# Gate bias and log-sigmoid taken 272 columns wide at the array, and scan operands written twice by the row loads

## Chip, core and metric

The kernel runs on one core of one Trainium2 chip, in float32. The metric is the device time of one execution in microseconds. Before the change it is 1172.42 us, the median of three runs (1170.26 to 1176.19).

In this text PE is TensorE, PEld its weight loads, DVE VectorE, ACT ScalarE, POOL GpSimd and SP the queue of SyncE that issues DMAs.

## The reference

One layer of a decoder trunk in which two groups of heads work side by side, followed by a final RMSNorm. There are 1024 prompt tokens and 8 sequences of 8 sample tokens, 1088 columns in all; the model width is 1024. Cut to what matters:

```python
xn   = rmsnorm(x, g_norm)
xm, zm, om, fh, qh, ih, zh = split(xn @ w_in)          # seven blocks of 1024 columns
xc   = silu(causal_conv(xm))                           # mLSTM group: 4 heads
q, k, v = xc_h @ w_q, xc_h @ w_k, xm_h @ w_v
gates = concat[q, k, v] @ w_gate + b_gate              # 8 numbers a token
ig, lf = gates[:, :4], log_sigmoid(gates[:, 4:])       # input gate, log of the forget gate
hm   = mlstm_scan(q, k, v, ig, lf)                     # b = cumsum(lf); m = running max
hm   = (layernorm(hm) * sigmoid(om) + m_skip * xc) * silu(zm)
oh   = hgrn2_scan(silu(qh), 1 - f, ih, log f)          # HGRN2 group: 8 heads, f from fh
oh   = rmsnorm(oh) * silu(zh)
y    = rmsnorm(x + concat[hm, oh] @ w_out)             # and the new states
```

The scan of the mLSTM needs, for each head, the row m over the tokens with m(t) = max(m(t-1) + lf(t), ig(t)), and the running sum b of lf. For the sample tokens each of the eight sequences starts anew from its own state.

## The kernel before

A float32 matmul is made of three passes over operands that are split in a high and a low part (`mm3`, lines 94 to 96: high times high, low times high, high times low). x is normalised, transposed and split into `XH` and `XL` once. W_in is read in blocks of 128 columns: for each, `in_block` loads the weights (`wraw`, line 140), casts them on ACT (`whi`) and subtracts on POOL or DVE (`wlo`, line 147), and multiplies them in three chunks of 384, 384 and 320 columns (PSUM tile `mm`, three buffers), each of which an evac function takes out.

The front does the eight xm blocks: convolution, q, k and v of the four mLSTM heads, and the gates. `gate_part` (L101 o<-qk,front) multiplies q and k of a head by the gate weights so that the result lies in four groups of 32 partitions: partition 32 j + r holds gate r (0 to 3 input, 4 to 7 forget) of columns 272 j to 272 j + 271. DVE adds the heads up in `GT`, columns 688 to 959 of the tile `front` (line 445). After the last head `gate_scan` makes the gate rows, and the trunk begins.

The trunk runs twelve jobs: H0, M0, H1, M1, H2, M2, H3, M3, H4 to H7. While the scan of one job runs (`hgrn_main` or `mlstm_main`), the input blocks of a following one (f, q, i, z of an H, om and zm of an M) are woven between its matmuls. `weave` deals them out: each `yield` of a main part states a time, and so much matmul work, times a ratio, is put in behind it. The ratio is the cost of a job's blocks divided by `HEAD` plus an `extra`. The order of PE is then fixed as written; that of the other engines comes from a scheduler that simulates times while the program is built. Each engine and each queue works strictly in its order.

In H0's stretch the input blocks are, in order, q, i and z of H0 itself and then om of M0. H0's own scan first forms Q, K and a burst of small matmuls (lv<-Q,K, line 101), then DVE forms seven levels of products (`products`: QK<-hq,f, line 1026; the levels 2, 4, 8 are one burst lv<-QK, the levels 16, 32, 64 the upper burst), DVE copies the results through masks into A (line 984 and 987), ACT copies A on (lines 1068 and 1075), and PE transposes KD (line 1132).

`gate_scan` is a generator: its first part runs at the end of the front, the others within H0's main part (`with_gates`). Before the change the first part stores `GT` to DRAM (`gd`, line 557), loads it back as two tiles with one head in a partition, `ig` and `y` (tile name gy, four partitions by 1088 columns, line 560), and adds the bias (line 561). The second part takes the log-sigmoid on ACT (lines 563 to 565) and DVE (line 566, `lf`, tile glf), copies `lf` to `t1` (tile gt) and `ig` to `y` (lines 571, 573), puts the sequence starts in, and scans m (line 575, tile gm). The third runs the second scan, b (line 583). `lm`, line 570, is the start of the sample sequences.

Of the kernel before, what the change touches and what calls it, by code (L numbers as in the profile page):

```python
# [15 lines left out]
P = 128  # L16
# [14 lines left out]
def hybrid_step(  # L31
# [276 lines left out]
    rd = dp.tile([4, T], F32, name="rd")  # L308
    mixd = dp.tile([15, P, T], F32, name="mixd")
    y0d = dp.tile([T, 512], F32, name="y0d")  # L310
    gd = dp.tile([P, 272], F32, name="gd")


    PAR = cp.tile([P, NPAR], F32, name="PAR")
# [231 lines left out]
        gate_part(h, parts, last)  # L546

    COLS = cp.tile([P, 9, 8], F32, name="COLS")
    bgt = cp.tile([4, 2], F32, name="bgt")
    m0t = cp.tile([4, 8], F32, name="m0t")  # L550
    nc.sync.dma_start(out=bgt, in_=b_gate[0].rearrange("(g h) -> h g", g=2))
    nc.sync.dma_start(out=m0t, in_=st_m[0].rearrange("b h -> h b"))

    def gate_scan():

        ig, y, lf, t1, m, b = [unit(s)[0:4, :T] for s in ("ig", "gy", "glf", "gt", "gm", "gb")]
        nc.sync.dma_start(out=gd, in_=GT)
        gv = gd.rearrange("(j r) t -> r j t", r=32)
        for g, dst in ((0, ig), (1, y)):
            nc.sync.dma_start(out=dst.rearrange("p (j t) -> p j t", t=272), in_=gv[4 * g:4 * g + 4])  # L560
            V.tensor_scalar(dst, dst, scalar1=bgt[:, g:g + 1], scalar2=None, op0=ALU.add)
        yield 1.0
        S.activation(t1, y, AF.Abs)
        S.activation(t1, t1, AF.Exp, scale=-1.0)
        S.activation(t1, t1, AF.Ln, bias=1.0)
        V.scalar_tensor_tensor(lf, y, 0.0, t1, op0=ALU.min, op1=ALU.subtract)
        lfs = lf[:, TP:T].rearrange("p (b c) -> p b c", c=8)[:, :, 0]
        igs = ig[:, TP:T].rearrange("p (b c) -> p b c", c=8)[:, :, 0]
        lm = small(8, "lm")
        V.tensor_tensor(lm[0:4, :], lfs, m0t, op=ALU.add)  # L570
        V.tensor_copy(t1, lf)
        V.memset(t1[:, TP:T].rearrange("p (b c) -> p b c", c=8)[:, :, 0], -1e30)
        V.tensor_copy(y, ig)
        V.tensor_tensor(y[:, TP:T].rearrange("p (b c) -> p b c", c=8)[:, :, 0], igs, lm[0:4, :], op=ALU.max)
        V.tensor_tensor_scan(m, t1, y, initial=0.0, op0=ALU.add, op1=ALU.max)
        yield 6.5
        G.memset(t1, 1.0)
        G.memset(t1[:, 0:TP].rearrange("p (b c) -> p b c", c=P)[:, :, 0], 0.0)
        G.memset(t1[:, TP:T].rearrange("p (b c) -> p b c", c=8)[:, :, 0], 0.0)
        st = lf[:, 0:TP].rearrange("p (b c) -> p b c", c=P)[:, 1:8, 0]  # L580
        V.tensor_tensor(st, st, m[:, 0:TP].rearrange("p (b c) -> p b c", c=P)[:, 0:7, 127], op=ALU.add)
        V.tensor_copy(lfs, lm[0:4, :])
        V.tensor_tensor_scan(b, t1, lf, initial=0.0, op0=ALU.mult, op1=ALU.add)
        V.tensor_tensor(y, b, m, op=ALU.subtract)
        nc.sync.dma_start(out=rd, in_=y)
        V.tensor_tensor(ig, ig, b, op=ALU.subtract)
        nc.sync.dma_start(out=o_pm[0, 0].unsqueeze(1), in_=m[:, TP - 1:TP])
        msl = small(8, "msl")
        V.tensor_copy(msl[0:4, :], m[:, TP:T].rearrange("p (b c) -> p b c", c=8)[:, :, 7])
        nc.sync.dma_start(out=o_sm[0].rearrange("b h -> h b"), in_=msl[0:4, :])  # L590
        yield 6.5
        ps = ps_o()
        for t in range(8):
            PE.transpose(ps[:, t * 8:t * 8 + 4], ig[:, t * P:t * P + P], ident[0:4, 0:4])
            PE.transpose(ps[:, t * 8 + 4:t * 8 + 8], m[:, t * P:t * P + P], ident[0:4, 0:4])
        for j in range(4):
            for o, src in ((64, ig), (68, m)):
                PE.matmul(ps[32 * j:32 * j + 32, o:o + 4], lhsT=src[:, TP + win(j):TP + win(j) + 32],
                          rhs=ident[0:4, 0:4], start=True, stop=True)
        V.tensor_copy(COLS.rearrange("p a b -> p (a b)"), ps[:, :72])  # L600
        S.activation(COLS[:, :, 4:8], COLS[:, :, 4:8], AF.Exp, scale=-2.0)
        yield 0.5

        co = unit("co")
        for kk in range(2):
            pt = ps_o()
            for k in range(4):
                PE.transpose(pt[:27, k * P:(k + 1) * P], CS[:, kk * 4 + k, :], ident)
            V.tensor_copy(co[:27, kk * 512:(kk + 1) * 512], pt[:27, :])
        nc.sync.dma_start(out=o_pconv[0, 0], in_=co[0:3, :DM])  # L610
        nc.sync.dma_start(out=o_sconv[0].rearrange("b j d -> (b j) d"), in_=co[3:27, :DM])
        yield 0.5
# [818 lines left out]
    with tc.manual_schedule(engines={mybir.EngineType.PE}):  # L1431
        for i, (kind, h) in enumerate(jobs[:-1]):
            main = (hgrn_main if kind == "H" else mlstm_main)(h)
            extra = 0.0
            if kind == "H" and i and jobs[i - 1][0] == "M":
                extra = 5.2
            if i == 0:
                main, extra = with_gates(main, gates), 14.0
            weave(islice(side, STEPS), main, us / (HEAD[kind] + extra))
        weave(side, hgrn_main(7), (us / 2 + EARLY * cost(45, 512)) / HEAD["H"])  # L1440
        for t in range(9):
# [100 lines left out]
```

## Time and profile before

| | |
|---|---|
| median of three runs | 1172.42 us (1170.26 to 1176.19) |
| profiled execution | 1167.87 us, its span 1166.1 us |
| mean granted TensorE clock | 0.992 |
| busy share of the span | PE 96%, PEld 91%, DVE 64%, ACT 40%, POOL 22% |
| gates, first to last instruction | 218.4 us (store of `gd`) to 278.9 us (COLS on ACT) |

The time of the profiled execution is its span and 1.8 us around it. A busy share is a mean over stages. A row of the timeline gives the start in us, the duration, the engine, the line of the kernel, the operation, the output and the inputs, and in brackets how long the engine had been idle before it and which work ended that.

### The profile page before, as it was taken

What the parts mean: (1) busy time and instruction counts of PE and PEld (TensorE: products, weight loads), DVE (VectorE), ACT (ScalarE), POOL (GpSimd) and SP (SyncE); (2) the same over time, 40 slices, a digit from 0 to 9 for tenths busy, and PEclk for the clock granted to TensorE, in tenths of its full rate; (3) what the DMA queues carried; (4) which work ended last, traced back from release to release, by engine and by line L of the source; (5) the groups of instructions that cost most, each with busy time, mean ns of one, the idle gap of its engine ahead of it and who ended that gap; (6) DMA issues with size and microseconds to landing.
All of it is one profiled execution on the core that took longest, in us unless ns stands there. A gap on an engine that the chain in (4) does not pass through costs nothing.

```text
span 1166.1 us, 22935 instructions
## 1 busy us (share of the span) xinstructions
PE 1124.4 (96%) x9251; PEld 1057.3 (91%) x9251; DVE 748.0 (64%) x1477; ACT 469.6 (40%) x1045; POOL 260.5 (22%) x402
## 2 busy tenths in 40 slices
PE   5889999998999999999999999999999999999997
PEld 5779999997999999999999999999999998878886
DVE  4665354485678657794679467878667586643543
ACT  5454454335532443235332553252423354343332
POOL 4352343101531044202530153102020200100000
PEclk9889999999999999999999999999999999999999
DMA  7234343213324242243224332322121155476662
GB/s 251 47 126 145 118 144 124 82 36 103 95 76 135 75 161 81 79 137 102 88 77 151 112 96 77 126 81 77 55 77 56 59 172 153 144 231 168 196 186 96
DMA packets 154060, 133.88 MB, mean 115 GB/s; under 512 B 11439, under 2 KB 130155, under 8 KB 153954
## 3 DMA queue, kind: packets, MB, share of 16 engines
q1 hardware_dynamic: 153954, 132.41, 36.5%
q8 instruction: 73, 1.20, 0.4%
q14 instruction: 33, 0.27, 0.1%
HBM read 93.96 MB, written 38.43 MB: 114 GB/s over the span
## 4 chain that ended last, share of the span: by engine, by line
PE 67%; ACT 4%; DMA 2%; DVE 2%; issue 1%; POOLq 0%; SPq 0%; DVEq 0%; ACTq 0%
PE mm L94 18%; PE mm L96 18%; PE mm L95 18%; PE lv L101 2%; ACT A L1075 1%; PE o L1178 1%; ACT A L1068 1%; PE o L1197 1%; DMA woraw<-in_w_out 1%; PE o L94 1%; PE o L95 1%; PE o L96 1%; PE o L1200 1%; DMA mraw<-mixd 1%; PE lv L712 1%
## 5 line engine op out<-in xcount | busy, mean ns | idle before, releaser
L94 PE MATMUL mm<-XH,whi 128*128 128x384 f32 (+1 forms) x1344 | 452.2, 337 | 3.2 <-DVE xml L470 2.0
L95 PE MATMUL mm<-XL,whi 128*128 128x384 f32 (+1 forms) x1344 | 440.6, 328 | 0.0
L96 PE MATMUL mm<-XH,wlo 128*128 128x384 f32 (+1 forms) x1344 | 440.1, 328 | 0.0
L94 PEld LDWEIGHTS mm<-XH,whi 128*128 128x128 f32 x1344 | 254.2, 189 | 6.9 <-DVE xml L470 2.2
L95 PEld LDWEIGHTS mm<-XL,whi 128*128 128x128 f32 x1344 | 254.3, 189 | 1.6 <-issue 1.3
L96 PEld LDWEIGHTS mm<-XH,wlo 128*128 128x128 f32 x1344 | 253.7, 189 | 0.0
L147 POOL TENSOR_TENSOR wlo<-wraw,whi 128x1024 fp32r<-128x1024 f32 x34 | 83.1, 2446 | 108.3 <-ACT whi L147 108.2
L147 ACT CAST whi<-wraw 128x1024 fp32r<-128x1024 f32 x56 | 58.8, 1051 | 104.8 <-PE mm L95 85.3
L944 POOL MEMSET A<- 128x288 f32 x8 | 2.7, 343 | 248.2 <-ACT A L1068 248.2
L94 PE MATMUL mm<-XH,mhi 128*128 128x512 f32 x144 | 57.2, 397 | 0.5 <-ACT mhi L1290 0.5
L96 PE MATMUL mm<-XH,mlo 128*128 128x512 f32 x144 | 56.3, 391 | 0.7 <-DVE mlo L1291 0.7
L95 PE MATMUL mm<-XL,mhi 128*128 128x512 f32 x144 | 56.1, 389 | 0.0
L1290 ACT CAST mhi<-mraw 128x1024 fp32r<-128x1024 f32 (+1 forms) x32 | 31.8, 997 | 60.1 <-PE mm L95 43.9
L1291 DVE TENSOR_TENSOR mlo<-mraw,mhi 128x1024 fp32r<-128x1024 f32 (+1 forms) x32 | 37.0, 1155 | 24.5 <-ACT mhi L1290 24.3
L892 DVE TENSOR_SCALAR f<-f,OML,LB 128x384 f32<-128x384 f32 (+1 forms) x24 | 33.8, 1407 | 28.5 <-ACT f L890 28.5
L470 DVE TENSOR_TENSOR xml<-mm,xmh 128x384 fp32r<-128x384 f32 (+1 forms) x24 | 12.3, 511 | 51.0 <-ACT XB L469 48.0
L1359 POOL TENSOR_TENSOR rs<-rs,mhalf 128x1 f32<-128x1 f32 (+1 forms) x9 | 4.9, 544 | 148.0 <-DVE rs L1358 148.0
L96 PE MATMUL mm<-woh,mlo 128*128 128x512 f32 x96 | 37.5, 390 | 0.4 <-DVE mlo L1291 0.4
L94 PE MATMUL mm<-woh,mhi 128*128 128x512 f32 x96 | 37.4, 389 | 0.0
L95 PE MATMUL mm<-wol,mhi 128*128 128x512 f32 x96 | 37.4, 389 | 0.0
L486 DVE SCALAR_TENSOR_TENSOR Y<-XB,PAR,Y 128x1112 f32<-128x1112 f32 x24 | 36.8, 1533 | 0.3
L199 POOL TENSOR_SCALAR oss<-oss 128x4 f32<-128x4 f32 (+1 forms) x24 | 4.6, 194 | 143.6 <-DVE oss L1148 143.6
(351 smaller groups left out, 2224.8 us busy)
## 6 DMA issues: line engine op xcount, KB each, us to landing
wraw<-in_w_in SPq DMA_DIRECT2D x56, 512.0 KB, 4.2
woraw<-in_w_out SPq DMA_DIRECT2D x16, 512.0 KB, 5.3
mraw<-mixd SPq DMA_DIRECT2D x16, 512.0 KB, 4.9
mraw<-mixd SPq DMA_DIRECT2D x16, 448.0 KB, 4.0
xcd<-XB SPq DMA_DIRECT2D x8, 544.0 KB
qkd<-qk SPq DMA_DIRECT2D x16, 272.0 KB, 3.5
xcr<-xcd SPq DMA_DIRECT2D x8, 544.0 KB
mixd<-xcr SPq DMA_DIRECT2D x8, 544.0 KB, 4.2
```

Of the source, the lines that this page charges most:

```text
L94: PE.matmul(out, lhsT=lh, rhs=rh, start=first, stop=False)
L95: PE.matmul(out, lhsT=lh, rhs=rl, start=False, stop=False)
L96: PE.matmul(out, lhsT=ll, rhs=rh, start=False, stop=last)
L101: i = PE.matmul(out, lhsT=lhsT, rhs=rhs, start=start, stop=stop)
L147: return S.copy(hi, raw), eng.tensor_tensor(lo, raw, f32(hi), op=ALU.subtract)
L470: evs.append(V.tensor_tensor(ml[:, t0:t0 + m], ps[:, :m], f32(mh[:, t0:t0 + m]), op=ALU.subtract))
L486: V.scalar_tensor_tensor(Y[:, :1112], XB[:, j:j + 1112], cw[:, 8 * j + ft:8 * j + ft + 1], Y[:, :1112], op0=ALU.mult, op1=ALU.add)
L712: PE.matmul(ps[:, u * P:(u + 1) * P], lhsT=k[:, j * P:(j + 1) * P], rhs=q[:, j * P:(j + 1) * P], start=True, stop=True)
L892: V.tensor_scalar(f[:, s], f[:, s], scalar1=OML[:, h:h + 1], scalar2=LB[:, h:h + 1], op0=ALU.mult, op1=ALU.add)
L1068: S.copy(dst, A32[32 * j:32 * j + 32, 0:256].rearrange("p (r e c) -> p r e c", e=2, c=32))
L1290: S.copy(hi[:, :w * n], raw[:, :w * n])
L1291: V.tensor_tensor(lo[:, :w * n], raw[:, :w * n], f32(hi[:, :w * n]), op=ALU.subtract)
```

## The change

Bias and log-sigmoid are taken on `GT` itself, where all eight gates of a quarter of the columns lie in one instruction of 272 columns on 128 partitions. The bias becomes a column of 128 partitions (`bgt`), filled by four loads of the eight numbers instead of one, after a memset to zero. The logs go to a new tile `lg`. `gd` holds two such tiles, gates and logs, and four loads instead of two write the rows: the logs to `lf` and to `t1`, the input gates to `ig` and to `y`. The two copies go. The stated times in `gate_scan` and the `extra` of H0 come down by 2.5.

```diff
-    gd = dp.tile([P, 272], F32, name="gd")
+    gd = dp.tile([2, P, 272], F32, name="gd")
...
-    bgt = cp.tile([4, 2], F32, name="bgt")
+    bgt = cp.tile([P, 1], F32, name="bgt")
+    G.memset(bgt, 0.0)
     m0t = cp.tile([4, 8], F32, name="m0t")
-    nc.sync.dma_start(out=bgt, in_=b_gate[0].rearrange("(g h) -> h g", g=2))
+    for j in range(4):
+        nc.sync.dma_start(out=bgt[32 * j:32 * j + 8, :], in_=b_gate[0].unsqueeze(1))
...
-        nc.sync.dma_start(out=gd, in_=GT)
-        gv = gd.rearrange("(j r) t -> r j t", r=32)
-        for g, dst in ((0, ig), (1, y)):
-            nc.sync.dma_start(out=dst.rearrange("p (j t) -> p j t", t=272), in_=gv[4 * g:4 * g + 4])
-            V.tensor_scalar(dst, dst, scalar1=bgt[:, g:g + 1], scalar2=None, op0=ALU.add)
+
+        lg = half("lg")
+        LF = lg[:, 0:272]
+        V.tensor_scalar(GT, GT, scalar1=bgt, scalar2=None, op0=ALU.add)
+        S.activation(LF, GT, AF.Abs)
+        S.activation(LF, LF, AF.Exp, scale=-1.0)
+        S.activation(LF, LF, AF.Ln, bias=1.0)
+        V.scalar_tensor_tensor(LF, GT, 0.0, LF, op0=ALU.min, op1=ALU.subtract)
+        for i, src in enumerate((GT, LF)):
+            nc.sync.dma_start(out=gd[i], in_=src)
+        for i, dst in ((1, lf), (1, t1), (0, ig), (0, y)):
+            nc.sync.dma_start(out=dst.rearrange("p (j t) -> p j t", t=272),
+                              in_=gd[i].rearrange("(j r) t -> r j t", r=32)[4 * i:4 * i + 4])
         yield 1.0
-        S.activation(t1, y, AF.Abs)
-        S.activation(t1, t1, AF.Exp, scale=-1.0)
-        S.activation(t1, t1, AF.Ln, bias=1.0)
-        V.scalar_tensor_tensor(lf, y, 0.0, t1, op0=ALU.min, op1=ALU.subtract)
...
-        V.tensor_copy(t1, lf)
...
-        V.tensor_copy(y, ig)
...
-        yield 6.5
+        yield 4.0
...
-                main, extra = with_gates(main, gates), 14.0
+                main, extra = with_gates(main, gates), 11.5
```

Lines behind the first scan lie 4 higher in the changed kernel (L900 becomes L904); the three activations of the gates keep the lines 563 to 565. What stands in the queues, in three places:

ACT, from the first third of H0's q block on (hq, evacuated from `mm`), before:

```order
L899 ACTIVATE hq_2047<-mm_2243 128x384
L899 ACTIVATE hq_2047<-mm_2270 128x384
L147 CAST whi_2355<-wraw_2237 128x1024
L899 ACTIVATE hq_2047<-mm_2297 128x320
L992 COPY Q_315_2342<-hq_2047 128x544
L957 COPY K_316_2345<-hk_2046 128x256
L957 COPY K_316_2345<-hk_2046 128x4x64
L912 COPY iT_2048<-mm_2359 128x128 x3
L563 ACTIVATE gt_2327<-gy_2325 4x1088
L564 ACT_TABLE_LOAD
```

and now, where the three activations and their table loads stand between the first and the second hq:

```order
L903 ACTIVATE hq_2051<-mm_2247 128x384
L563 ACTIVATE lg_2334<-front_341 128x272
L564 ACT_TABLE_LOAD
L564 ACTIVATE lg_2334<-lg_2334 128x272
L565 ACT_TABLE_LOAD
L565 ACTIVATE lg_2334<-lg_2334 128x272
L903 ACT_TABLE_LOAD
L903 ACTIVATE hq_2051<-mm_2274 128x384
L147 CAST whi_2366<-wraw_2241 128x1024
L903 ACTIVATE hq_2051<-mm_2301 128x320
L996 COPY Q_316_2353<-hq_2051 128x544
L961 COPY K_317_2356<-hk_2050 128x256
```

DVE at the same place, from the first hq on, before:

```order
L900 TENSOR_TENSOR hq_2047<-hq_2047,mm_2243 128x384
L561 TENSOR_SCALAR ig_2324<-ig_2324,bgt 4x1088
L561 TENSOR_SCALAR gy_2325<-gy_2325,bgt 4x1088
L900 TENSOR_TENSOR hq_2047<-hq_2047,mm_2270 128x384
L147 TENSOR_TENSOR wlo_2356<-wraw_2237,whi_2355 128x1024
L900 TENSOR_TENSOR hq_2047<-hq_2047,mm_2297 128x320
L993 TENSOR_TENSOR Q_315_2342<-hq_2047,f_2045 128x544
L957 COPY K_316_2345<-hk_2046 128x256
```

and now, with the four small operations on the loaded rows ahead of the weight split and of the third hq; the scan gm (L579) has moved up behind Sf, ahead of all level products:

```order
L904 TENSOR_TENSOR hq_2051<-hq_2051,mm_2247 128x384
L566 SCALAR_TENSOR_TENSOR lg_2334<-front_341,lg_2334 128x272
L904 TENSOR_TENSOR hq_2051<-hq_2051,mm_2274 128x384
L576 TENSOR_TENSOR lm_2448<-glf_2330,m0t 4x8
L586 COPY glf_2330<-lm_2448 4x8
L577 MEMSET gt_2331 4x8
L578 TENSOR_TENSOR gy_2329<-ig_2328,lm_2448 4x8
L147 TENSOR_TENSOR wlo_2367<-wraw_2241,whi_2366 128x1024
L904 TENSOR_TENSOR hq_2051<-hq_2051,mm_2301 128x320
L997 TENSOR_TENSOR Q_316_2353<-hq_2051,f_2049 128x544
```

DVE around the last level product, for which the upper burst waits (QK of level 64, the second of the two QK<-hq,f here), before:

```order
L1026 TENSOR_TENSOR QK_2703<-hq_2047,f_2045 128x512
L1029 TENSOR_TENSOR Sf_2341<-Sf_2341,f_2045 128x16x32
L1031 TENSOR_TENSOR f_2045<-f_2045 128x16x32
L960 TENSOR_TENSOR QK_2722<-hk_2046,Sf_2341 128x4x64 x2
L1108 TENSOR_TENSOR iT_2048<-hk_2046,Sf_2341 128x128
L1026 TENSOR_TENSOR QK_2722<-hq_2047,f_2045 128x512
L1029 TENSOR_TENSOR Sf_2341<-Sf_2341,f_2045 128x8x64
```

and now, where a weight split and the last third of z have come to stand behind it:

```order
L1030 TENSOR_TENSOR QK_2702<-hq_2051,f_2049 128x512
L1033 TENSOR_TENSOR Sf_2352<-Sf_2352,f_2049 128x16x32
L991 COPY_PREDICATED A_314_2350<-mk_371,lv_2620 128x72x2
L1035 TENSOR_TENSOR f_2049<-f_2049 128x16x32
L964 TENSOR_TENSOR QK_2720<-hk_2050,Sf_2352 128x4x64 x2
L991 COPY_PREDICATED A_314_2350<-mk_372,lv_2620 128x36x4
L1030 TENSOR_TENSOR QK_2720<-hq_2051,f_2049 128x512
L147 TENSOR_TENSOR wlo_2692<-wraw_2516,whi_2691 128x1024
L904 TENSOR_TENSOR z_2053<-z_2053,mm_2595 128x320
```

PE's order is the same but for four places in H0's stretch, where a group of six matmuls of an input block changes places with the lower burst, the transposes of iT, the first outputs of H0, or the conv-state transposes.

## The prediction

> **What bounds the kernel now.** First the page's busy times and the chain that ended last.
>
> ```profile
> PE 1124.4 (96%) x9251; PEld 1057.3 (91%) x9251; DVE 748.0 (64%) x1477; ACT 469.6 (40%) x1045; POOL 260.5 (22%) x402
> PE 67%; ACT 4%; DMA 2%; DVE 2%; issue 1%; POOLq 0%; SPq 0%; DVEq 0%; ACTq 0%
> ```
>
> PE is busy 96% of the span, so only a pause of PE that goes, or comes, moves the end. Next PE's waits from 215 to 300 us, where the gates lie beside head H0 and the entry into M0 (columns: total, times, longest; a wait of 1.0 for z follows below).
>
> ```profile
> PE lv L101 <- DVE QK L1026: 2.3, 1, 2.3
> PE lv L1132 <- ACT A L1075: 2.2, 1, 2.2
> PE lv L1159 <- DVE osq L1150: 0.4, 1, 0.4
> PE o L1197 <- DVE co L609: 0.3, 1, 0.3
> PE o L1228 <- DVE osq L1150: 0.3, 1, 0.3
> ```
>
> All but one want DVE's work, and so does the ACT one at one remove: its copies of A wait for DVE's last masked copy. The windows show DVE full while PE pauses, and a lower PEclk after the pause (columns: PE, PEld, DVE, ACT, POOL busy, clock, DMA).
>
> ```profile
> 250.00:255.00 5.00, 4.00 (x130) 3.70 (x130) 5.00 (x7) 1.39 (x2) 0.00 (x0) 1.00 0.26 76
> 265.00:270.00 5.00, 3.45 (x42) 3.28 (x42) 5.00 (x11) 2.12 (x7) 0.00 (x0) 0.66 0.00 0
> 270.00:275.00 5.00, 2.81 (x23) 2.57 (x21) 0.61 (x3) 4.16 (x12) 0.34 (x1) 1.00 0.01 3
> ```
>
> **The cost before.** The timeline of DVE, where the gate work sits in its queue:
>
> ```profile
> 217.93 0.44 DVE L445 TENSOR_TENSOR front<-front,o 128x272 f32<-128x272 f32 x1 [6.54 <-PE o L101]
> 222.11 0.78 DVE L561 TENSOR_SCALAR ig<-ig,bgt 4x1088 f32<-4x1088 f32 x1 [2.03 <-DMA ig<-gd]
> 227.61 1.23 DVE L147 TENSOR_TENSOR wlo<-wraw,whi 128x1024 fp32r<-128x1024 f32 x1 [3.37 <-ACT whi L147]
> 228.75 0.48 DVE L900 TENSOR_TENSOR hq<-hq,mm 128x320 f32<-128x320 f32 x1
> 230.79 0.73 DVE L1010 TENSOR_TENSOR f<-f 128x544 f32<-128x544 f32 x1
> 237.38 1.28 DVE L566 SCALAR_TENSOR_TENSOR glf<-gy,gt 4x1088 f32<-4x1088 f32 x1 [4.35 <-ACT gt L565]
> 240.15 0.16 DVE L574 TENSOR_TENSOR gy<-ig,lm 4x8 f32<-4x8 f32 x1
> 265.82 0.68 DVE L1026 TENSOR_TENSOR QK<-hq,f 128x512 f32<-128x512 f32 x1
> 270.23 0.30 DVE L987 COPY_PREDICATED A<-mk,lv 128x128 f32<-128x128 uint8 x1
> ```
>
> From 237.38 to the row at 265.82 DVE has no idle: it is one run of 28.4 us that began late, because L566 waited 4.35 for the log-sigmoid on ACT. PE reached the product written by the row at 265.82 at 264.21 and waited. What PE did, and the same stage two heads later (H2), which has no gates beside it:
>
> ```profile
> 230.76 0.65 PE L101 MATMUL lv<-Q,K 128*32 128x64 f32 x32
> 253.68 0.44 PE L94 MATMUL mm<-XH,whi 128*128 128x384 f32 x1 [1.00 <-DVE z L900]
> 263.21 1.00 PE L101 MATMUL lv<-QK 128*32 128x32 f32 x64
> 266.55 1.08 PE L101 MATMUL lv<-QK 128*32 128x64 f32 x32 [2.34 <-DVE QK L1026]
> 274.10 0.66 PE L1132 MATMUL lv<-CF,iT 128*128 128x128 f32 x4 [2.19 <-ACT A L1075]
> 524.75 1.22 PE L101 MATMUL lv<-QK 128*32 128x32 f32 x96
> 529.88 0.66 PE L1132 MATMUL lv<-CF,iT 128*128 128x128 f32 x4 [0.48 <-ACT A L1075]
> ```
>
> From the start of the upper burst (levels 16 to 64) to the second group of KD transposes H0 takes 274.10 - 263.21 = 10.89 us, H2 529.88 - 524.75 = 5.13, with the same matmuls between. The 5.76 are 2.34 of the one pause, 2.19 - 0.48 = 1.71 of the other, and 1.71 of the slow stretch.
>
> **The change, part by part.** *DVE loses* the two copies L571 and L573 and one of the two bias adds L561; the other, and L566, run 272 wide instead of 1088. The rows of ACT and of SP's queue on which the new path is priced:
>
> ```profile
> 212.50 0.40 ACT L543 ACTIVATE qk<-mm 128x272 f32<-128x272 f32 x1 [0.29 <-PE mm L96]
> 219.00 0.49 ACT L899 ACTIVATE hq<-mm 128x384 f32<-128x384 f32 x1 [6.10 <-PE mm L96]
> 223.16 0.49 ACT L899 ACTIVATE hq<-mm 128x384 f32<-128x384 f32 x1 [3.67 <-PE mm L96]
> 229.86 0.83 ACT L957 COPY K<-hk 128x256 f32<-128x256 f32 x2
> 232.51 1.28 ACT L564 ACT_TABLE_LOAD   x1
> 233.81 1.12 ACT L564 ACTIVATE gt<-gt 4x1088 f32<-4x1088 f32 x1
> 239.66 1.05 ACT L147 CAST whi<-wraw 128x1024 fp32r<-128x1024 f32 x1 [1.85 <-issue]
> 218.40 0.32 SPq L557 DMA_DIRECT2D gd<-front  x1
> 220.13 0.27 SPq L560 DMA_DIRECT2D ig<-gd  x1
> 220.50 0.27 SPq L560 DMA_DIRECT2D gy<-gd  x1
> ```
>
> *The new path to the gate rows.* The bias add is at most the 0.44 of L445 on the same shape; it is over before ACT's first hq (219.00 + 0.49 = 219.49), so it costs nothing. Then on ACT: three activations at 0.40 (the 272-wide row) with a table load of 1.30 (233.81 - 232.51) after each: Abs ends 219.89, Exp 221.59, Ln 223.29, the sigmoid table is back at 224.59. The second hq leaves ACT 1.4 late, at 225.1; its buffer is next wanted by the second i chunk, behind the burst at 230.76, so that hides it. The subtraction on DVE takes 0.44: 223.73. SP stores `lg` 0.03 later; the first load follows the store by 220.13 - 218.40 = 1.73, the fourth by 3 x 0.37 more, and its data come 222.11 - 220.13 = 1.98 after its issue: 223.76 + 1.73 + 1.11 + 1.98 = 228.6.
>
> *The added wait.* `lm` and the small `gy` operation now stand in DVE's queue ahead of the split of z's weights (227.61 before) and the third hq (228.75). They release the queue at 228.7, so both run 1.1 late. Who waits: z's weights are needed when z starts, where ACT casts the next ones (239.66), so nine microseconds hide it. But ACT's Q and K copies follow the third hq, the K copies ended at 230.69, and PE's first burst of H0 started at 230.76, at once. So PE pauses there: **+1.1**. The trace has no such wait; its bounds are 0 (data 1.1 faster: the split would not move) and +3.3 (data 2.2 slower, as the 4.2 us to landing of a 512 KB weight load in the page's list of DMA issues, below). I take 1.1, since its row is the same load from the same tensor.
>
> *The stretch that goes.* DVE finishes f at 231.5 + 1.1 = 232.6 and then has no reason to idle: `glf`, `gt`, `gy` and `ig` are all there. Of its 28.4 us, 2.8 (237.38 to 240.15) fall away, and a weight split and the last third of z (1.23 and 0.48, by the rows of the same shapes) now follow the row at 265.82 instead of leading it, while two masked copies come in (288 and 144 wide: at most 3.4 times the 0.30 of the 128-wide one, 1.0). That row moves to about 232.6 + 25 = 258, against PE's need at 264.2 + 1.1 - 1.0. The wait for z goes: **-1.00**. The upper burst should then look as in H2: **-5.76**; what remains late there is ACT's copying of A, 0.48. The outputs of H0 and the conv-state transposes move six matmuls apart from each other in PE's order, which should take the 0.34 wait for `co`: **-0.3**.
>
> *Cheap parts.* SP issues three more small loads of b_gate at 23.5 and four row loads instead of two. Each takes 0.3, so at the start the QKV weights, the state rows and w_gate start 0.9 later. Cover: POOL idles 2.67 before the first user of those weights.
>
> ```profile
> 23.51 0.26 SPq L551 DMA_DIRECT2D bgt<-in_b_gate  x1
> 39.97 1.27 POOL L393 TENSOR_TENSOR wql<-wqkv,wqh 128x512 fp32r<-128x512 f32 x1 [2.67 <-ACT wqh L391]
> wraw<-in_w_in SPq DMA_DIRECT2D x56, 512.0 KB, 4.2
> ```
>
> Without that cover it would be 0.9. The memset of `bgt` on POOL lies before the first x has landed. The weight load behind the gate rows on SP waits for the split, as before, and has until 239.66.
>
> **Sum:** +1.1 - 1.0 - 5.8 - 0.3 = -6.0 us. Against the profiled execution's 1167.87 this gives 1161.9. The three runs shown have the median 1172.42 (1170.26 to 1176.19), 4.6 above it; the forecast for a median is 1172.4 - 6.0 = **1166.4**, -0.51%. Its bounds: with no new wait and the two later DVE waits of that stage (0.4 and 0.3) gone too, -7.8; with the 3.3 wait and a slow stretch that stays, -2.1.
>
> [...]
>
> **Rivals.** *A slow stretch at another place.* The clock fell to 0.66 after the 2.34 pause and cost 1.71. The new pause at 230.8 sits in front of a burst of small matmuls, as that one did. If it does the same, 1166.4 + 1.7 = 1168.1. Against it: the clock stayed at 1.00 after the 1.00 pause and after the 2.19 one. [...]
>
> *The gate rows land late, and it is slower.* DVE's queue stands at `lm` until they land; each microsecond beyond 1.98 is one more on PE. It breaks even at 1.98 + 6.0 = 8.0. The 512 KB weight loads take 4.2; at 10 us the time would be 1174.4. The gate rows are 17 KB a load.
>
> *Nothing moves.* If ACT, not DVE, sets PE's two large pauses, only the z wait and `co` go and the new wait stays: 1172.2. ACT was waiting for DVE before A, so I think little of it.
>
> *More goes.* The two later waits go as well, no new pause: 1164.6.
>
> **Chances.** The forecast 0.64, slow stretch 0.12, gate rows somewhat late (up to 4 us of data time, 1168.4) 0.08, slower 0.04, nothing 0.05, more 0.07. About 0.5%, 5.9 us, is what a measurement of this kernel can tell from no change, and the forecast lies on that edge: a little over half of its 0.64 (0.35) and "more" (0.07) count as faster, 0.42; slower 0.04; the rest 0.54. The range: 1172.42 - 7.8 = 1164.6 to 1172.42 - 2.1 = 1170.3, each widened by 2.2, the way from the median to the lowest run: 1162 to 1172.5.
>
> **What would show it.** Right: ACT's three 272-wide activations near 0.4; the row loads issued at 225.5 to 226.6; DVE idle before `lm` until about 227.5; a new PE pause near 1.1 at the first burst of H0; DVE's last level product near 258; no PE wait for QK or z, 0.5 for A, full clock from 260 to 275; the stages after 300 us alike but 6 earlier. Wrong: a pause of over 3 at that first burst, or a slow stretch after it; a wait for QK that stays; a change in the first 100 us.

## The result, and the profile after

The changed kernel took 1163.69 us (median of five runs, 1162.91 to 1166.35); the kernel before, measured with it, 1172.42 (five runs, 1170.26 to 1176.19). The ratio on record is 0.9947, with an interval of 0.9927 to 0.9968; these two medians alone would give 0.9926, just outside it, and where the difference comes from stays open. A second comparison, twelve runs of the changed kernel against 23, gave 1165.43 against 1170.05, 0.9961 (0.9942 to 0.9980). So the gain is between 0.2 and 0.7%, 4.6 to 8.7 us by the medians, about where the prediction put the edge of what can be told from no change. Of the two profiled executions the span went from 1166.1 to 1161.9.

In the changed kernel A is copied by ACT at L1079, the second KD transposes are L1136, the products L1030; lm is L576.

The page's busy times after:

```profile
PE 1122.9 (97%) x9251; PEld 1055.8 (91%) x9251; DVE 744.4 (64%) x1474; ACT 467.4 (40%) x1045; POOL 259.5 (22%) x403
```

Hardly anything of the change can be seen here. It shows in PE's waits from 215 to 300 us (total, times, longest):

```profile
PE lv L101 <- DVE K L961: 2.2, 1, 2.2
PE lv L1136 <- ACT A L1079: 0.6, 1, 0.6
PE o L1232 <- DVE osq L1154: 0.3, 1, 0.3
```

Six waits of 6.5 us together, the one for z among them, have become three of 3.1. The waits for QK, z, co and the early osq are gone, the one for A is down from 2.2 to 0.6, and one is new: 2.2 us at the first burst. The windows (PE, PEld, DVE, ACT, POOL busy, granted clock, DMA):

```profile
265.00:270.00 5.00, 4.35 (x32) 4.11 (x32) 0.14 (x1) 4.72 (x14) 0.34 (x1) 1.00 0.02 4
270.00:275.00 5.00, 5.00 (x60) 4.72 (x59) 1.84 (x7) 3.31 (x6) 2.35 (x1) 1.00 0.02 6
```

The clock stays at 1.00 and DVE is through with its run before 265. The four steps on PE's timeline, with M0's first matmul last:

```profile
232.14 0.65 PE L101 MATMUL lv<-Q,K 128*32 128x64 f32 x32 [2.18 <-DVE K L961]
263.56 1.24 PE L101 MATMUL lv<-QK 128*32 128x32 f32 x96
268.72 0.66 PE L1136 MATMUL lv<-CF,iT 128*128 128x128 f32 x4 [0.65 <-ACT A L1079]
297.21 0.61 PE L716 MATMUL lv<-q,k 128*128 128x128 f32 x4
```

And the same row in the kernel before:

```profile
303.78 0.61 PE L712 MATMUL lv<-q,k 128*128 128x128 f32 x4
```

The new path to the gate rows, on ACT, SP's queue and DVE:

```profile
218.53 0.42 ACT L563 ACTIVATE lg<-front 128x272 f32<-128x272 f32 x1
222.00 0.43 ACT L565 ACTIVATE lg<-lg 128x272 f32<-128x272 f32 x1
222.94 0.32 SPq L568 DMA_DIRECT2D gd<-lg  x1
224.71 0.27 SPq L570 DMA_DIRECT2D glf<-gd  x1
225.78 0.25 SPq L570 DMA_DIRECT2D gy<-gd  x1
217.07 0.44 DVE L445 TENSOR_TENSOR front<-front,o 128x272 f32<-128x272 f32 x1 [6.55 <-PE o L101]
226.90 0.16 DVE L576 TENSOR_TENSOR lm<-glf,m0t 4x8 f32<-4x8 f32 x1 [2.07 <-DMA glf<-gd]
227.99 0.07 DVE L577 MEMSET gt<- 4x8 f32 x1 [0.73 <-DMA gt<-gd]
228.71 0.16 DVE L578 TENSOR_TENSOR gy<-ig,lm 4x8 f32<-4x8 f32 x1 [0.66 <-DMA gy<-gd]
230.35 0.48 DVE L904 TENSOR_TENSOR hq<-hq,mm 128x320 f32<-128x320 f32 x1
256.99 0.67 DVE L1030 TENSOR_TENSOR QK<-hq,f 128x512 f32<-128x512 f32 x1
```

DVE stands three times at a small operation that waits for a load to land (lm, gt and gy), and the third hq comes only after that.

### The profile page after: what moved, and what is told of

Read it like the earlier page. It is cut to its first block, busy times and chain, and to the rows that moved or that the text cites. A ratio compares the mean times of both kernels' runs of the same rounds, so it can differ in the third digit from the quotient of the medians.

```text
span 1161.9 us, 22940 instructions
## 1 busy us (share of the span) xinstructions
PE 1122.9 (97%) x9251; PEld 1055.8 (91%) x9251; DVE 744.4 (64%) x1474; ACT 467.4 (40%) x1045; POOL 259.5 (22%) x403
## 4 chain that ended last, share of the span: by engine, by line
PE 78%; DVE 8%; ACT 5%; DMA 5%; issue 2%; SPq 0%; POOL 0%; POOLq 0%; DVEq 0%; ACTq 0%
PE mm L94 22%; PE mm L95 21%; PE mm L96 21%; PE lv L101 2%; DMA woraw<-in_w_out 1%; DMA mraw<-mixd 1%; ACT A L1079 1%; DMA RB<-rd 1%; ACT A L1072 1%; PE o L1182 1%; PE o L94 1%; PE o L96 1%; PE o L95 1%; PE o L1201 1%; PE o L1204 1%
```

## A measure that leaves the scatter out

The start of the program and its end scatter from execution to execution. DVE's L445, the last step before the gates, began between 215.81 and 218.14 us in the fourteen traces of this study, without order by kernel. It goes with the clock: the first stretch at half clock, near 40 us, lasts 6.8 us in six of the traces, and there L445 began at 217.07 to 218.14; it lasts 3.4 us in the other eight, and there it began at 215.81 to 217.40. Behind M0 the two traces drift apart at the loads of RB, which are sometimes on the path and sometimes not (rows of the chain of waits; first the changed kernel, then the kernel before):

```profile
423.59 0.45 PE lv L716 x4
530.27 6.33 DMA RB<-rd
550.51 0.45 PE lv L716 x4
```

```profile
430.24 0.44 PE lv L712 x4
556.44 0.44 PE lv L712 x4
```

The lead is 6.65 us at M1 and 5.93 at M2. So most of what follows is read from inside one stretch: from the start of H0's first burst (lv<-Q,K) to M0's first matmul (lv<-q,k), with the pause ahead of the burst, the wait of PE just before it, beside it. In the changed kernel that is 297.21 - 232.14 = 65.07 and 2.18, in the kernel before 303.78 - 230.76 = 73.02 and 0: 5.77 us less in all.

## The experiments

Each ratio is against runs of the kernel before that were taken together with the run in question.

| run | pause | burst to M0 | sum | ratio to before |
|---|---|---|---|---|
| before | 0 | 73.02 | 73.02 | 1 |
| changed | 2.18 | 65.07 | 67.25 | 0.9947 (0.9927 to 0.9968) |
| changed, again (e9) | 2.27 | 65.07 | 67.34 | 0.9961 (0.9942 to 0.9980) |
| changed, third (e11) | 2.35 | 65.01 | 67.36 | one run |
| row steps behind Sf (e1) | 0 | 65.12 | 65.12 | 0.9935 (0.9913 to 0.9957) |
| wide, loads once (e2) | 1.62 | 66.48 | 68.10 | 0.9941 (0.9920 to 0.9962) |
| the same, again (e12) | 0 | 66.42 | 66.42 | 0.9960 (0.9945 to 0.9976) |
| log-sigmoid on rows (e3) | 0 | 71.88 | 71.88 | 0.9997 (0.9981 to 1.0014) |
| changed, old weave (e4) | 2.37 | 68.08 | 70.45 | 0.9970 (0.9953 to 0.9986) |
| before, new weave (e5) | 0 | 71.86 | 71.86 | 0.9990 (0.9974 to 1.0006) |
| e1 with the old weave (e6) | 0 | 66.58 | 66.58 | 0.9934 (0.9910 to 0.9957) |
| e1, ballast of five (e7) | 0 | 69.69 | 69.69 | one run |
| e1, ballast of six (e8) | 0 | 70.98 | 70.98 | one run |
| e1, subtractions on POOL (e10) | 0 | 67.51 | 67.51 | 0.9954 (0.9936 to 0.9972) |

An interval of the ratios is 1.8 to 2.8 us of time to each side. It tells the kernels with the wide log-sigmoid and the new weave from the kernel before and from e3 (from e3 only just: 0.9980 against 0.9981), not from each other; there the trace has to speak, and that is one trace for each row of the table.

### Which part brings the gain: the log-sigmoid on rows (e3)

```diff
-        S.activation(LF, GT, AF.Abs)
-        S.activation(LF, LF, AF.Exp, scale=-1.0)
-        S.activation(LF, LF, AF.Ln, bias=1.0)
-        V.scalar_tensor_tensor(LF, GT, 0.0, LF, op0=ALU.min, op1=ALU.subtract)
...
+        S.activation(t1, b, AF.Abs)
+        S.activation(t1, t1, AF.Exp, scale=-1.0)
+        S.activation(t1, t1, AF.Ln, bias=1.0)
+        V.scalar_tensor_tensor(lf, b, 0.0, t1, op0=ALU.min, op1=ALU.subtract)
...
+        V.tensor_copy(t1, lf)
```

Only the gates are stored; three loads bring the input gates to ig and y and the forget gates to b, a tile that is free until the second scan.

> The log-sigmoid taken back: bias on 128 x 272, three row loads (ig, the f gates, and ig again into gy), but Abs, Exp, Ln and the subtraction on 4 x 1088 rows, and the copy glf to gt on VectorE. Theory (the long stages of 4 x 1088 on ScalarE behind the iT copies were what held the first scan): VectorE again waits 4 us and more for ScalarE's Ln with only one copy (0.6 us) saved of what stood before the scan, so no pause before lv<-Q,K, but a QK wait of 1.3 to 2.0 us before the upper burst and an A wait above 1 us: 1 to 3 us below the kernel before, 1167 to 1171 against 1170 to 1172. Rival (the narrow bias and the copies on VectorE were the cost, ScalarE's chain was hidden): no QK wait, and the time at or below that of the changed kernel, 1162 to 1164.

PE's waits from 215 to 300 us in this kernel:

```profile
PE lv L101 <- DVE QK L1030: 3.2, 2, 2.1
PE lv L1136 <- ACT A L1079: 2.4, 1, 2.4
PE o L1232 <- DVE osq L1154: 0.3, 1, 0.3
```

The larger piece of the QK wait, on PE's timeline:

```profile
254.98 0.46 PE L101 MATMUL lv<-QK 128*32 128x32 f32 x32 [2.12 <-DVE QK L1030]
```

DVE again waited 4.35 us for ACT's Ln. The QK wait is back, in two pieces of 1.07 and 2.12 us, and with it the A wait and a stretch at half clock from 256.4 on. But it is not where it was forecast: both pieces lie in the lower burst (from 250.69), and the upper burst, at 267.32, has none. In this kernel the scheduler put the second scan and its two subtractions (244.26 to 251.55 on DVE) ahead of the two products that the lower burst waited for. The stretch takes 71.88 us, 1.14 below the kernel before, and the ratio is 1 within its interval. The theory holds in its mechanism, DVE late because of the log-sigmoid on rows; it was wrong in the place and the size of the wait, and its 1 to 3 us of gain in time did not show. The rival, that the narrow bias and copies were the cost, falls.

### Which part brings the gain: the weave (e4, e5, e6)

```diff
-        yield 4.0
+        yield 6.5
...
-                main, extra = with_gates(main, gates), 11.5
+                main, extra = with_gates(main, gates), 14.0
```

That is e4: the old weave in the changed kernel. e5 makes the opposite edit to the kernel before, e6 makes this one to e1.

> The changed kernel with the two numbers of the old weave (6.5 in place of 4.0 behind the first scan, 14.0 in place of 11.5 for H0), which moves some groups of the i and z products on TensorE against H0's bursts and touches nothing else. Theory (the gain is ScalarE's and VectorE's, the weave costs nothing): the stretch from the upper burst to the second KD transposes stays 5.2 us, 0.5 us or less of difference in time, 1163.2 to 1164.2. Rival (the order of the array's groups carries part of the gain): a wait for QK or z of 1 us or more comes back, 1165 to 1167.

PE's first burst in it (timeline), and two windows of 3.41 us (the columns as above):

```profile
231.38 0.65 PE L101 MATMUL lv<-Q,K 128*32 128x64 f32 x32 [2.37 <-DVE K L961]
```

```profile
229.51:232.92 3.41, 1.53 (x83) 1.54 (x84) 3.38 (x7) 1.83 (x6) 0.00 (x0) 1.00 0.52 152
232.92:236.33 3.41, 3.41 (x13) 3.41 (x12) 3.41 (x9) 0.00 (x0) 2.13 (x6) 0.50 0.03 6
```

Three us more from the burst to M0, and about the time that the rival has, 1167.02; but no wait for QK or z came back, and 1.7 of the three, by an estimate (half of the 3.41 us that PE worked at 0.50), are a stretch at half clock. It follows a pause that the weave does not touch: up to the burst PE's matmuls are the same, in the same order, as in the changed kernel. That left two readings, and e5 and e6 were to part them.

> The kernel before with the two numbers of the new weave (4.0 behind the first scan, 11.5 for H0) and nothing else: log-sigmoid on 4 x 1088, two loads, copies. Theory (the log-sigmoid on the rows is the cost, the weave at most 1 us): the pause for z (1.00 us) may go or move, the QK wait of about 2 us, the A wait of about 2 us and 3 us of half clock stay; from the first burst to M0's first transposes 72 to 73 us against 73.02 in the kernel before and 65.1 in the changed one; the ratio 0.9985 to 1.000. Rival (the run with the old weave was 3 us slower than the changed kernel because of the order on TensorE): 70 us or less from the first burst to M0, ratio near 0.997.

> The kernel with the row steps queued behind Sf, and the old weave (6.5, 14.0). With the old weave the changed kernel took 68.1 us from its first burst to M0 against 65.1; 1.7 us of these were a stretch of 3.3 us at half clock behind a pause of 2.37 us. Theory (the half clock follows the pause, the weave itself costs under 1 us in small waits): no pause, no half clock, 65.8 to 66.2 us from the first burst to M0, about 1 us above the kernel with the row steps behind Sf, ratio near 0.994. Rival (the old order of the groups costs the 3 us by itself): 67.5 us or more, ratio 0.996 or above.

e5 took 71.86: the new weave alone is worth 1.16 us, a little more than the theory's 1. e6 took 66.58 without pause or half clock: the old weave costs 1.46 against e1, more than the 0.7 to 1.1 expected, less than half of the rival's 3. Nearly all of it sits in one place. From the second KD transposes to M0 the kernel before takes 303.78 - 274.10 = 29.68 us, the changed one 297.21 - 268.72 = 28.49.

The account of the change is then, from the burst to M0: 73.02, 71.86 with the new weave, 71.88 with the wide bias and a third load as well, 65.07 with the wide log-sigmoid and both operands of the first scan loaded. The last step is the gain, -6.81, and the pause takes 2.18 of it back. That step takes away one copy on DVE as well as the rows' log-sigmoid; what the copies are worth follows with e12.

### The pause at the first burst (e1)

`behind` makes an instruction stand after another one in the queue; `ctxs["sf"]` is the copy of f into Sf, which follows Q and K.

```diff
+        ctxs["sf"] = V.tensor_copy(hv(Sf, T, 1)[:, :, 0, :], ...)
...
-        V.tensor_tensor(lm[0:4, :], lfs, m0t, op=ALU.add)
-        V.memset(t1[...], -1e30)
+        for i in (V.tensor_tensor(lm[0:4, :], lfs, m0t, op=ALU.add), V.memset(t1[...], -1e30)):
+            behind(i, ctxs["sf"])
```

> The changed kernel, with the addition of lm and the memset of gt queued behind the copy of f into Sf on VectorE, so that nothing of the gates stands ahead of Q and K of H0's first burst. Theory (the 2.18 us pause of TensorE before lv<-Q,K is VectorE standing at lm, gt and gy until the four row loads land, 226.90 to 229.21): the third hq and Q are made 2 us earlier, the pause falls to 0.3 us or less, the scans' 1.2 us and more of slack behind them hold, the upper burst still finds its QK, and the time is about 2 us below the changed kernel's 1163.7, near 1161.7, a ratio to the kernel before near 0.993. Rival (slack is conserved): the first scan now starts behind f and later against the array, the products are late instead and a wait for QK of 1 to 2 us comes back before the upper burst, with the time of the changed kernel, 1163 to 1165. Second rival (the pause is ScalarE's hq or the weight split wlo, not the rows): the pause stays above 1 us and nothing moves.

DVE and PE in it (its lines are one higher again):

```profile
227.35 0.48 DVE L905 TENSOR_TENSOR hq<-hq,mm 128x320 f32<-128x320 f32 x1
229.26 0.15 DVE L576 TENSOR_TENSOR lm<-glf,m0t 4x8 f32<-4x8 f32 x1
229.35 0.65 PE L101 MATMUL lv<-Q,K 128*32 128x64 f32 x32
```

No wait at lm, gt or gy any more, no pause on PE, and 65.12 us behind it: the 2.2 us are gained whole and nothing gives them back, so both rivals fall. The pause was DVE standing at the small operations on the loaded rows. In time, 1162.80 (1161.31 to 1164.75) and a ratio of 0.9935 agree with that and do not prove it.

### Two loads or four (e2, e12)

```diff
-        for i, dst in ((1, lf), (1, t1), (0, ig), (0, y)):
+        for i, dst in ((1, lf), (0, ig)):
...
+        V.tensor_copy(t1, lf)
+        V.tensor_copy(y, ig)
```

> The wide half of the change alone: bias and log-sigmoid on 128 x 272, but only two row loads (glf, ig), and the two copies glf to gt and ig to gy are made by VectorE as before (0.71 us each). Theory (what stands at the queue's head is paid by the burst, what stands behind Q and K is covered): only lm, which needs the first load alone, is left ahead of the weight split; the copies lie behind Q and K, where 5.9 us of cover (last product over at 257.66, upper burst at 263.56) take their 1.4 us. Pause before lv<-Q,K 0 to 0.5 us in place of 2.18, no QK wait: about 2 us below the changed kernel, near 1161.7. Rival (loading twice is a gain of its own): VectorE's 1.4 us come on top, 1165 to 1166. Second rival (the landing of one load, 2.19 us, sets the pause, not the number of loads): pause 1.5 to 2.2, time that of the changed kernel.

A pause of 1.62, as the second rival has it, and an A wait of 2.1, which nobody expected. SP's queue showed that the first load was issued 3.67 us behind the store, against 1.73 to 2.04 elsewhere, so the same kernel ran again.

> The wide half alone (two row loads, two copies on VectorE) once more, since in its first trace the store of the gates took 3.67 us before the load behind it was issued, against 1.77 to 2.04 in nine other traces. Theory (the pause of 1.62 us there was that late store; one load ahead of the weight split lands in time, and the 1.4 us of copies are paid at the A wait): store to load about 1.9 us, pause before lv<-Q,K 0 to 0.2 us, A wait 2.0 to 2.2 us, 66.3 to 66.6 us from the first burst to M0, so about 0.8 us better than the changed kernel over both and 1.4 us worse than the row steps behind Sf; ratio 0.993 to 0.995. Rival (a load that stands at the queue's head always costs its landing): pause 1.5 us or more again with an ordinary store.

SP's queue in e2, then SP's queue and DVE's lm in e12, then PE's largest wait there:

```profile
224.01 0.32 SPq L568 DMA_DIRECT2D gd<-lg  x1
227.68 0.27 SPq L570 DMA_DIRECT2D glf<-gd  x1
```

```profile
221.67 0.32 SPq L568 DMA_DIRECT2D gd<-lg  x1
223.57 0.27 SPq L570 DMA_DIRECT2D glf<-gd  x1
225.48 0.15 DVE L576 TENSOR_TENSOR lm<-glf,m0t 4x8 f32<-4x8 f32 x1 [1.92 <-DMA glf<-gd]
```

```profile
PE lv L1138 <- ACT A L1081: 2.0, 1, 2.0
```

With an ordinary store (1.90 us to the first load) there is no pause, as the theory has it, and the two copies, which hold DVE's queue for 1.27 us, come out as 1.31 more at the A wait (1.96 against 0.65) and 1.30 more to M0. So loading twice is worth 1.3 us of DVE, but as the change has it, with the rows at the head of the queue, it costs 2.2: the wide half alone, 66.42, is 0.8 us better than the changed kernel's 67.25, and e1 with both, 65.12, better than either. By time the three are not to be told apart; e12's ratio, 0.9960, even lies above the forecast 0.993 to 0.995. Why the store of e2 took longer stays open.

### How much cover DVE has in H0 (e7, e8)

Cover is work that an engine can do late without anyone waiting for it. To measure it, e1 gets five subtractions more, into a tile that is no longer needed, and the next product is held behind them.

```diff
+        for _ in range(5):
+            ctxs["bal"] = V.tensor_tensor(lf, b, m, op=ALU.subtract)
         V.tensor_tensor(y, b, m, op=ALU.subtract)
...
-            V.tensor_tensor(Qn[...], ...)
+            i = V.tensor_tensor(Qn[...], ...)
+            if "bal" in ctxs:
+                behind(i, ctxs.pop("bal"))
```

In e8 the loop runs six times.

> The kernel with the row steps behind Sf, and five subtractions of 4 x 1088 on VectorE (1.2 us each, into a dead tile) behind the second scan, ahead of the last products: to measure the cover there. Last product over at 254.96 and upper burst at 260.77 leave 5.8 us; the ballast is 6.0 us, and a weight split, a z product and two small ones (1.9 us) that stood behind the last product come ahead of it. Theory (VectorE's work there is covered to 5.8 us and paid above): a QK wait of 1.8 to 2.4 us; no half clock behind it if it stays at or under the 2.18 us that had none before. Rival (VectorE's work there is paid in full): 6 us more than without ballast. Rival (a pause above 1.5 us always brings half clock): 1.7 us more on top.

> As the kernel with five subtractions, with six (7.2 us). Theory: each further subtraction is paid in full, QK wait 3.0 to 3.6 us, and behind it 3.3 us at half clock (1.7 us lost), as behind the pauses of 2.34 and 2.37 us; about 3 us more than with five. Rival (the half clock belongs to the order of work or to the loss of A, not to the length of the pause): full clock behind the pause, 1.2 us more than with five.

PE's waits in e7, then in e8:

```profile
PE lv L1141 <- ACT A L1084: 3.5, 1, 3.5
PE lv L101 <- DVE QK L1033: 1.6, 1, 1.6
```

```profile
PE lv L101 <- DVE QK L1033: 2.8, 2, 2.1
PE lv L1141 <- ACT A L1084: 2.0, 1, 2.0
```

The QK wait came near its forecast (1.6 for 1.8 to 2.4). But the A wait rose from 0.65 to 3.49, and of 6.0 us of ballast 4.57 arrived at M0. The cover of 5.8 us, read at the upper burst, was no cover: the second KD transposes wait for A, which hangs on DVE's queue through Vs and the last masked copy, and there the slack is already used up, as the 0.65 says: ACT's VL waited for DVE's Vs 0.71 us in e1 and 2.88 in e7. For the 1.4 that did not arrive there are two moves, which fit by size but were not tested: hq<-hq,f, which holds DVE's queue for 1.20 (260.63 to 261.83 in e10), came to stand behind the last masked copy, and ACT's om, 0.37, ahead of VL. With six, 1.29 more for 1.2 of ballast, the rival's figure; but the half clock of the theory came too: behind the pauses of 0.62 and 2.14 it lasted 3.4 us, and the A wait, 1.5 shorter than in e7, took most of that up.

### The grid of the half clock (e9, e11)

In some traces the granted clock is half for a while behind a pause, in others not. Windows of one microsecond show where a stretch at half clock begins. Two of the kernel before:

```profile
61.00:62.00 1.00, 0.00 (x0) 0.00 (x0) 1.00 (x2) 0.00 (x0) 0.99 (x1) 0.80 0.12 15
266.00:267.00 1.00, 0.45 (x20) 0.45 (x23) 1.00 (x2) 0.00 (x0) 0.00 (x0) 0.70 0.00 0
```

At 0.80 the half clock fills 0.4 of the microsecond, so it begins at 61.6; at 0.70 it fills 0.6, so the other begins at 266.4. Those are 204.8 us apart. Read in this way, the stretches of the fourteen traces up to 1150 us last 3.40 to 3.42 us or 6.82 to 6.84. 204.8 is 60 times 3.413, and in e3, e4, e5 and e8 the second stretch and the late one lie 57, 51, 60 and 60 times 3.413 us apart, each to 0.02 us. So in these traces the stretches begin on the lines of a grid of 3.413 us, which stood differently in each execution: in the three of the changed kernel the second stretch began at 60.76, 61.56 (e9) and 60.66 us (e11). Between 200 and 300 us every stretch lasts one step. So the windows of the grid ahead of each can be read. First the kernel before, then e8, then e7, which had a pause of 3.49 us:

```profile
262.99:266.40 3.41, 1.13 (x66) 0.69 (x64) 3.38 (x8) 2.80 (x9) 0.00 (x0) 1.00 0.52 148
266.40:269.81 3.41, 3.26 (x40) 3.09 (x41) 3.41 (x7) 1.28 (x4) 0.00 (x0) 0.50 0.00 0
```

```profile
262.57:265.98 3.41, 0.98 (x64) 0.84 (x64) 3.38 (x7) 1.41 (x5) 0.00 (x0) 1.00 0.02 6
...
269.39:272.81 3.42, 1.50 (x11) 1.25 (x10) 0.34 (x2) 3.30 (x11) 0.34 (x1) 1.00 0.02 5
```

```profile
264.90:268.31 3.41, 1.64 (x13) 1.40 (x11) 1.99 (x5) 2.92 (x9) 0.06 (x1) 1.00 0.02 5
268.31:271.73 3.42, 1.70 (x13) 1.70 (x14) 0.23 (x1) 3.10 (x10) 0.28 (x1) 1.00 0.00 0
```

A window with PE busy for 0.98 to 1.53 us was followed by one at half clock (five cases between 200 and 300 us, e4's above the last of them). 3.49 us of pause, cut by a line of the grid into windows of 1.64 and 1.70, had none behind them. So here the length of a pause alone did not decide.

Nor did the busy time of the window alone. The last row of e8 has 1.50, right behind a window at half clock, and full clock after it; e12 has 1.55 (264.66 to 268.07) and full clock. Elsewhere in the program windows with more work were followed by half clock: 1.69 in e12 (1036.07 to 1039.49), 1.79 in e4 (1038.47 to 1041.88), and 2.35 to 2.75 ahead of the stretch near 40 us in six traces. What PE does in the window may count as well: the five cases hold 39 to 84 matmuls, a burst of small ones, the two rows of e7 13 each. That was not tested, and the windows of e12 and e4 past 1036 us, with 6 and 8 wide matmuls, do not fit it.

> The changed kernel once more, unaltered. In the traces so far the half clock comes in whole windows of 3.413 us on a grid that runs through the whole execution, and follows a window in which TensorE was busy for 0.45 or less; windows of 0.48 and more had none, with one at 0.44 without. The changed kernel's pause of 2.2 us before lv<-Q,K lay across a line of that grid (0.57 and 0.79 busy). Theory (the grid's phase decides): where the grid leaves 1.9 us or more of the pause in one window, which is about half of all phases, the trace shows 3.4 us at 0.50 behind the pause and 1.7 us more from the burst to M0 (66.8 in place of 65.07); elsewhere 65.1; its executions lie in two groups, near 1163 and 1165. Rival (the changed kernel is free of it, the length of the pause or the place decides): 65.1 whatever the phase.

> The changed kernel a third time, for another phase of the grid. Theory: half clock behind the first burst's pause if and only if a window of the grid holds 1.9 us or more of it (TensorE busy 0.45 or less); with it 66.8 us from the burst to M0, without 65.1. Rival: 65.1 in any phase.

Both ran without half clock there (65.07 and 65.01). In both a line of the grid cut the pause: the emptiest window had PE busy for 1.56 us in e11 (227.91 to 231.33) and 1.89 in e9 (228.81 to 232.23). So neither met the condition of 0.45, e11 only just, and theory and rival are not told apart by these two. The 12 times of e9 (1161.62 to 1169.29) do not fall into the two groups that were expected. Between 200 and 300 us the half clock followed windows that were busy for 0.29 to 0.45, elsewhere also windows of 0.50 to 0.81 (1.69 to 2.75 us, above); so over the whole trace neither the 0.45 nor the "if and only if" holds.

e4, which is the changed kernel up to there, had the half clock behind a pause of 2.37 us, and e11 had none behind 2.35. The same work and nearly the same pause, with another grid: that the phase decides here is well supported, by one case against three. What it decides by is open. The windows of e4 and e11 are idle for nearly the same time, 1.88 and 1.86 us, but e4's ends behind the burst of small matmuls (83 in all) and e11's ahead of it (9 wide ones).

### Less work for DVE, on POOL (e10)

```diff
-        V.tensor_tensor(y, b, m, op=ALU.subtract)
+        G.tensor_tensor(y, b, m, op=ALU.subtract)
...
-        V.tensor_tensor(ig, ig, b, op=ALU.subtract)
+        G.tensor_tensor(ig, ig, b, op=ALU.subtract)
```

> The kernel with the row steps behind Sf, and the two subtractions behind the second scan (gy<-gb,gm and ig<-ig,gb, 1.27 us each on VectorE) given to GpSimd. The ballast of 6.0 us at that place cost 4.6 us, so most of VectorE's work there is paid at the A wait of the second KD transposes and 1.4 us is covered. Theory (VectorE's queue up to Vs sets ScalarE's VL and so A): the A wait falls from 0.65 us to 0 to 0.3, a gain of 0.4 to 0.65 us, 64.5 to 64.8 us from the first burst to M0, not to be seen in the ratio (0.9925 to 0.994). Rival (the A wait is ScalarE's own chain of copies behind the upper burst): the A wait stays at 0.6 to 0.7 and nothing moves. Rival (GpSimd's subtractions slow VectorE beside them): the A wait grows.

The timeline of POOL and DVE, and PE's largest wait:

```profile
245.87 2.89 POOL L589 TENSOR_TENSOR gy<-gb,gm 4x1088 f32<-4x1088 f32 x1 [11.11 <-DVE gb L588]
248.74 2.71 POOL L591 TENSOR_TENSOR ig<-ig,gb 4x1088 f32<-4x1088 f32 x1
246.30 5.42 DVE L965 TENSOR_TENSOR QK<-hk,Sf 128x256 f32<-128x256 f32 x2
```

```profile
PE lv L1137 <- ACT A L1080: 2.9, 1, 2.9
```

The third case came. Two products that take 0.74 us together in e1 took 5.42 while POOL worked. DVE lost 4.7 us and saved 2.4; the A wait grew by 2.3, and M0 came 2.4 later. That the A wait follows DVE's queue one for one, the theory's first half, is borne out by the sign that was not wanted.

## Why the prediction was right, and where it was off

It forecast 1166.4 and -6.0 us; the medians were 1163.69 and -8.7, then 1165.43 and -4.6; from the bursts to M0 the traces give -5.77. Term by term:

- *The upper burst to the second KD transposes, -5.76:* 268.72 - 263.56 = 5.16 for 5.13 forecast, -5.73. The cause is as given: DVE's run began late because it waited for ACT's log-sigmoid on the rows (e3 puts that wait back, and PE pays for it, though at the lower burst). One part of the term is less sure than it looked: the 1.71 of the slow stretch hang on where the grid stands in an execution. All three traces of kernels with the log-sigmoid on rows (before, e3, e5) had it, e3 at the lower burst; that another may lack it is inferred from e7, not seen.
- *The wait for z, -1.0:* from the first burst to the upper one 32.45 before, 31.42 after, -1.03.
- *The pause at the first burst, +1.1:* mis-sized, 2.18 (2.27 and 2.35 in the two other traces). Place and mechanism were right (e1). The step that failed is the landing, taken as 1.98 us behind the issue of the fourth load, from the first load of a pair. The chain up to there was right (fourth load 8.71 us behind L445, forecast 8.67), but its data came 2.93 after the issue: the loads follow one another at 0.37 in the queue and are each used some 0.7 to 1.1 apart. The split that now stands behind adds 0.33.
- *co, -0.3:* mis-sized, -1.19 from the second KD transposes to M0. All of it is the weave: by their own rows e5, with the new weave, takes 28.5 us there and e6, with the old, 29.7. The other early wait, for osq, went as well, which the prediction only had as a bound; the two waits are 0.72 of the 1.19, and the other 0.47 show in no wait.
- *The sum:* that it comes within 0.23 of -5.77 is in part luck, since the pause was 1.1 too small and co 0.9 too small, and the two cancel.
- *Right without a price:* ACT's activations 0.42 and 0.43, and the log-sigmoid's last one at its end 5.36 us behind the start of L445 (222.43 - 217.07) for a forecast 5.36 (223.29 - 217.93), so each of the two table loads on the way cost 1.29, from its start to the next activation (218.97 to 220.26 and 220.71 to 222.00), for the row's 1.30; the last level product at 256.99 for 258; no QK wait, no z wait, 0.65 for A, full clock from 260 to 275; rows issued from 224.71 (forecast 225.5, and the whole front 0.86 early). A change in the first 100 us was named as a sign of error. It was there, and it is scatter: L445 began at 217.93 in the kernel before and at 215.90 in e5, which has the same front.
- *The rival of a slow stretch at the new place* (0.12) did not come in three traces of the changed kernel and came in e4's. e4 and e11, with the same work up to the burst and pauses of 2.37 and 2.35 us, differ in where the grid stands. So its chance is one of an execution, not of the kernel.
- *The other rivals:* the rows landed 2.19 to 2.93 us after their issue, far from the 8.0 at which the change breaks even. That nothing moves, because ACT sets the pauses, falls with the QK wait. That more goes, without the new pause, is what e1 does (65.12 in all for 67.25).

What stays open: why the difference of the two spans, 4.2, is below that of the medians, 8.7 and 4.6. At M0 the changed kernel leads by 6.6 us, 0.9 of them from before L445; 2.4 of the lead are lost again behind M0, where the chain of the changed kernel runs over loads of RB and of the output part. One trace a kernel does not show how often such loads fall on the path.

## What to carry to other kernels

A small operation that waited for a transfer cost here what stood behind it in its engine's queue, not what it takes itself: a few operations of 4 x 8, 0.07 to 0.16 us each, cost 2.2 us, and an ordering edge that put them behind the work that the array needed took that away. The slack of an engine is the least one over all who wait for it; 5.8 us at the next burst meant nothing while a later step already waited 0.65. And a term of a sum that rests on a clock drop in one trace should be looked for in a second trace before it is counted as a gain: e4 had the drop behind its pause of 2.37 us, e11 none behind 2.35.

## What the hardware did that was not expected

- In the fourteen traces the half clock (0.50) came in stretches of 3.40 to 3.42 us or twice that, on a grid of 3.413 us: in e4 those at 58.84 and 1041.88 us begin 983.04 us apart, 288 times 3.4133. Between 200 and 300 us it followed windows in which the array was busy for 0.98 to 1.53 of 3.41 us, while others with 1.50 to 1.96 had none behind them; what decides is open. In e4 PE worked through all 3.41 us of it, so that it cost 1.7 us there, an estimate.
- Two DVE products of 128 x 256 took 5.42 us in place of 0.74 beside two POOL subtractions of 2.89 and 2.71 us (e10). Why is not shown.
- From the issue of a small store to that of the load that waits for it, 1.73 to 2.04 us in thirteen traces and 3.67 in one (e2), enough for a pause of 1.6 us on the array.
